# Conv transposes and query transposes later, one more empty step in the banded tail, raw output weights in general slots

## The chip, the cores and the metric

The kernel runs on one core of one Trainium2 chip, as one program without collectives. The metric is the device time of one execution in microseconds; the time before is the median of three executions, 1818.41 us (1817.18 to 1819.79). The engines of the core are TensorE (PE; its weight loads are listed as PEld), VectorE (DVE), ScalarE (ACT), GpSimd (POOL) and SyncE (SP), which here only issues DMAs. L709 means line 709 of the kernel before.

## The reference

Two layers of a backbone block over 1024 latent tokens and 256 context tokens, width 1024, all in float32:

```python
h  = rmsnorm(x, norm_w) * (1 + scale) + shift          # adaLN; the same for the context, hc
pl = split(h @ w_in)                                   # 14 parts: four branches and their gates
ya = softmax(q k^T) v   # A: latent attention, 4 heads, keys of context and latent tokens
yb = softmax(q k^T) v   # B: the same with rms-normed q, k; 4 heads, 2 key heads
yc = ...                # C: windowed: 128 tokens to either side, the context, and a sink term in the sum
yd = ...                # D: centred conv of 5 taps, silu, bidirectional state-space scan
x  = x + gate * (concat(ya, yb, yc, yd, each times silu of its gate) @ w_out)
```

The context gets the same update in the first layer only; the result is the final RMSNorm of x. In C the sink adds exp(sink) to the sum of exponentials by which the values are divided.

## The kernel before

Activations lie with features on partitions and tokens along the free axis, in three groups of tokens: the context (256) and two latent groups (512 each). Each float32 product is made of three passes of TensorE: operands are split into a high part (hi) and a low part (lo), and `mm3` adds hi·hi, lo·hi and hi·lo (L128, L129, L130). So each weight matrix that comes by DMA as raw float32 (`wfm_raw`, `wtm_raw`, `wo_raw`) is turned into hi by a cast and into lo by a subtraction before TensorE can use it.

A layer runs in this order: the input projection as a list of jobs (`in_proj`), the state-space branch spread over them, attention (branch 1, then 0, then 2; each with two pairs of heads), and the output projection (`out_proj`).

**Flushes.** Work that needs TensorE but depends on another engine is not issued at once. It is put on a list `soon` as `[delay, function]`. After each group of products `flush` issues the entries whose delay is 0 or less, to stand behind the group's last product, and takes 1 off the others. A conv job ends in `conv_fin`: VectorE adds five taps into cv (for the latent tokens) and cvc (context), ScalarE and VectorE make cth from them (L701, L702), and `turn` transposes cth in blocks of 128 on TensorE (L709, to ps_sxt), copies it to xbt on ScalarE (L711) and stores it (L712). A conv has ten such blocks. A `tm` job makes queries, keys and values with tokens on partitions; each pair of token tiles has a second half of its work, whose transposes (L781, to ps_qkt) wait for POOL's qkv (L736). It runs three pairs behind; the three that are left at the end go onto `soon` (L1029).

**Attention.** A unit is one branch, one pair of heads and one token group. It goes through blocks of keys: scores (ps_st), exponential to P on ScalarE (L1231), values (ps_acc, L1239); VectorE and POOL add the P's to ac (L1248, L1254). Beside it, for a later unit, scores in the other layout (ps_s) are reduced to maxima mp (L1148), which the softmax needs as a shift. What a unit still has to do is its tail, a list of steps that the next unit's blocks take, one for each block, or two while the list has more than six (in `main`): the output copy, two empty steps, `token_sums` (ps_sum, L1300; then asum, with a reciprocal, L1309), an empty step, and `finish`, which transposes the reciprocals (ps_rt, L1313), sends them through DRAM to be spread over partitions (rb) and multiplies (y, L1323). TensorE's order in attention is that of the program; other engines' orders come from the scheduler's estimates.

**Buffers.** `Slot` takes one of 35 general places of 4 KB a partition, freed by hand. `bg` is a ring of six such buffers, shared by P, by raw weights, and by the split outputs yh and yl.

**Output weights.** There are eight. In the last units of a layer `late(keep)` gives four steps per weight: issue the load (if enough slots are free), nothing, then two halves of cast and subtraction on VectorE (L1571, L1572). `out_proj` fetches what is missing with `split_w` (L288 to L292: DMA, cast on ScalarE, subtraction on VectorE).

Of the kernel before, what the change touches and what calls it, by code (L numbers as in the profile page):

```python
# [17 lines left out]
P = 128  # L18
# [39 lines left out]
def hybrid_block(ctx, tc, x, ctxt, c_t, w_fm, w_tm, w_mod, b_gate, p_col, p_row, w_qu, w_kvu, w_out,  # L58
# [572 lines left out]
    def in_proj(L, ht, need_ctx, side, follow, both, begun, make_last):  # L631
# [51 lines left out]
        def conv_fin(i, xp, has_ctx):  # L683
            xl, xc = xp
            w = halfw[:, i * 5:(i + 1) * 5]
            vl = Slot([P, NLAT], F32, "cv")
            parts = [(xl.t, vl.t, NLAT)]
            if has_ctx:
                parts.insert(0, (xc, tm((P, NCTX), name="cvc"), NCTX))
            for src, v, n in parts:  # L690
                nc.vector.tensor_scalar(out=v, in0=src, scalar1=w[:, 2:3], scalar2=halfb[:, i:i + 1],
                                        op0=ALU.mult, op1=ALU.add)
                for d in (-2, -1, 1, 2):
                    a, b = max(0, -d), n - max(0, d)
                    nc.vector.scalar_tensor_tensor(out=v[:, a:b], in0=src[:, a + d:b + d], scalar=w[:, d + 2:d + 3],
                                                   in1=v[:, a:b], op0=ALU.mult, op1=ALU.add)
            xl.free()
            for (lo, n) in (GROUPS if has_ctx else GROUPS[1:]):
                v = parts[0][1] if lo < NCTX else vl.t[:, lo - NCTX:lo - NCTX + n]
                th = tm(name="cth")  # L700
                nc.scalar.activation(out=th[:, :n], in_=v, func=AF.Tanh)  # L701
                nc.vector.scalar_tensor_tensor(out=th[:, :n], in0=th[:, :n], scalar=1.0, in1=v, op0=ALU.add, op1=ALU.mult)  # L702
                if i >= 2:
                    nc.sync.dma_start(out=d_xbc[i][:, lo:lo + n], in_=th[:, :n])
                if i < 4:
                    def turn(th=th, lo=lo, n=n):
                        pst = ps("S2", name="ps_sxt")
                        for t in range(n // P):
                            nc.tensor.transpose(pst[:, t * P:(t + 1) * P], th[:, t * P:(t + 1) * P], ident)  # L709
                        tt = tm(name="xbt")  # L710
                        nc.scalar.copy(tt[:, :n], pst[:, :n])  # L711
                        nc.sync.dma_start(out=d_xbt[i][:, lo:lo + n], in_=tt[:, :n])  # L712
                    soon.append([0, turn])
            vl.free()

        halfw = const([P, 30])
# [244 lines left out]
        for ji, j in enumerate(jobs):  # L961
            if ji < 2:
                continue
            w, nxt = nxt, None
            if j[4] is not None:
                j[4]()
            if ji + 1 < len(jobs):
                nxt = fetch(L, jobs[ji + 1])
            pieces, units = [], 0
            if ji >= len(jobs) - 2:  # L970
                if ji == len(jobs) - 2:
                    flush(ins, True)
                    for f in up:
                        f()
                    while side:
                        side.pop(0)()
                    first = follow(res)
                first.pop(0)()
                if ji == len(jobs) - 1:
                    pieces, units = first, 8 * len(j[2])  # L980
            if j[0] in ("fm", "conv"):
                def each():
                    nonlocal units
                    for _ in range(-(-len(pieces) // units) if units else 0):
                        pieces.pop(0)()
                    units -= 1

                if j[0] == "conv":
                    xp, ev = conv_prep(j[3], GROUPS[0] in j[2])
                else:  # L990
                    ev = j[3]
                for lo, n in j[2]:
                    if todo:
                        run(-(-len(todo) // n_ssd))
                        n_ssd -= 1
                    p, ins = products(ht, w, lo, n, "S2" if pieces else "MX", each)
                    ev(lo, n, p)
                    if side and SIDE0 <= ji < SIDE1:
                        side.pop(0)()
                    flush(ins)  # L1000
                if j[0] == "conv":
                    conv_fin(j[3], xp, GROUPS[0] in j[2])
                if side and ji >= 14:
                    side.pop(0)()
            else:
                whi = [u[0].t.rearrange("p (k c) -> p k c", c=256) for u in w]
                wlo = [u[1].t.rearrange("p (k c) -> p k c", c=256) for u in w]
                pend, due = [], 0
                for ti, t in enumerate(j[2][::2]):
                    p = ps("MX", name="ps_tm")  # L1010
                    for u in range(2):
                        for k in range(8):
                            ins = mm3(p[:, u * 256:u * 256 + 256], hh[k].tile(t + u), hl[k].tile(t + u),
                                      whi[k // 4][:, k % 4, :], wlo[k // 4][:, k % 4, :], k == 0, k == 7)
                    pend.append(tm_pair(j[1][0], j[1][1], t, p))
                    if ti >= 1:
                        pend[-2][0]()
                    if ti >= THIRD:
                        with tc.issue_after(ins.ins):
                            pend[-1 - THIRD][1]()  # L1020
                    flush(ins)
                    if side:
                        side.pop(0)()
                    due += UP_RATE.get(ji, 0)
                    while due >= 1 and up:
                        due -= 1
                        up.pop(0)()
                pend[-1][0]()
                soon.extend([0, f[1]] for f in pend[-THIRD:])  # L1029
            for u in w:  # L1030
                free_all(u)
            if j[5] is not None:
                j[5]()
# [4 lines left out]
    def attention(L, res, need_ctx, y, late, ahead):  # L1038
# [164 lines left out]
        def main(op, gi, steps, tail):  # L1203
# [107 lines left out]
            def finish():  # L1311
# [9 lines left out]
                    nc.sync.dma_start(out=rb[h * 64:h * 64 + 64, :n],  # L1321
                                      in_=dr[h * nt:(h + 1) * nt, :].rearrange("t q -> (t q)").unsqueeze(0).to_broadcast([64, n]))
                nc.vector.tensor_tensor(out=y[br * 2 + op["pair"]](lo, n), in0=rb[:, :n], in1=o[:, :n], op=ALU.mult)  # L1323
            return tail + [output, idle, idle, lambda: [token_sums(h) for h in range(2)], idle, finish]

        def idle():
            pass
# [202 lines left out]
    for L in range(DEPTH):  # L1530
        need_ctx = L < DEPTH - 1
        if L > 0:
            both, begun = [fetch(L, j) for j in first_two], {}
            ht = [], [], []
            add_half(ht)
            add_half(ht)
            for g in order(L)[:2]:
                for part in range(4):
                    make_ht(L, xs, ht, {}, g, part)

        def make_last():
            for part in range(4 if L else 0):
                make_ht(L, xs, ht, {}, order(L)[2], part)

        side = mod_g
        if L + 1 < DEPTH:
            load_params(L + 1)
            a, mod_g = mod_steps(L + 1)
            side = side + a
        else:  # L1550
            side = list(side)
        y, wo, gen, y_pairs = {}, [], [], {}

        def ahead():
            y_pairs[2] = y_pair(y, 2)

        def late(keep):

            st = []

            def first():
                if len(wo) < 8 and len(free_slots) >= 2 + keep:
                    raw = bg(name="wo_raw")
                    nc.sync.dma_start(out=raw, in_=w_out[L, len(wo)])
                    st.extend([raw, Slot([P, 1024], F32R, "wo_hi"), Slot([P, 1024], F32R, "wo_lo")])
                    wo.append(st[1:])

            def half(j):
                if st:
                    js = slice(j * 512, (j + 1) * 512)  # L1570
                    nc.vector.tensor_copy(st[1].t[:, js], st[0][:, js])  # L1571
                    nc.vector.tensor_tensor(out=st[2].t[:, js], in0=st[0][:, js], in1=f32(st[1].t[:, js]), op=ALU.subtract)  # L1572
            return [first, lambda: None, lambda: half(0), lambda: half(1)]

        def follow(res):
            for i in range(2):
                y[6 + i] = res["ssd"].y[i]
            gen.append(attention(L, res, need_ctx, y, late, ahead))
            return next(gen[0])

        res = in_proj(L, ht, need_ctx, side, follow, both, begun, make_last)
        y_slots, tail = next(gen[0])
        xs = out_proj(L, y, need_ctx, wo, tail, y_slots + res["ssd"].y_slots, y_pairs)
# [85 lines left out]
```

## Time and profile before

| | |
|---|---|
| median of 3 executions | 1818.41 us |
| the profiled execution | 1815.12 us, of it 1813.3 in the span of the trace |
| mean granted TensorE clock | 0.985 of full speed |
| busy: PE, DVE, POOL, ACT | 1718.6, 1141.4, 785.7, 734.4 us |
| DMA | 231.61 MB moved, 128 GB/s in the mean |

Busy times of engines overlap. PE is busy 95% of the span; what a change can take away lies in the rest, or in stretches where the clock is lower. The profile of this one execution says where. All durations below are from it; its time stands 3.3 us under the median.

### The profile page before, as it was taken

How to read it: one execution, taken by the hardware profiler on the slowest of the kernel's cores; microseconds unless marked ns; L12 is line 12 of the kernel's file. 1: busy time of each engine (PE TensorE's matmuls, PEld its weight loads, DVE VectorE, ACT ScalarE, POOL GpSimd, SP SyncE). 2: the span in 40 equal slices, each digit the busy share in tenths (PEclk: the TensorE clock that was granted, in tenths of full speed). 3: DMA queues.
4: the chain of work that ended last, by engine and by line, in shares of the span. 5: the costliest groups of instructions: out<-in, count | busy, mean ns of one | idle time of the engine just before them, and what ended most of it. 6: DMA issues, size and time to landing. Idle time of an engine off the chain costs nothing.

```text
span 1813.3 us, 27884 instructions
## 1 busy us (share of the span) xinstructions
PE 1718.6 (95%) x9658; PEld 1340.2 (74%) x9658; DVE 1141.4 (63%) x2294; ACT 734.4 (40%) x2048; POOL 785.7 (43%) x735
## 2 busy tenths in 40 slices
PE   6999999999989999998999889999999999999798
PEld 4667888899976566675787668888998656666586
DVE  6866965274347665668545677862753777656853
ACT  5432434333224554555423333343322355555431
POOL 2312643042325767665323233540342477666522
PEclk9999999999999999999999989999999999999999
DMA  9474333156566331322511434241668643221521
GB/s 317 142 235 138 123 103 125 50 191 197 190 181 167 109 101 35 99 81 88 185 59 41 132 120 140 82 146 39 205 186 258 175 120 89 56 67 36 172 74 58
DMA packets 130480, 231.61 MB, mean 128 GB/s; under 512 B 13826, under 2 KB 74628, under 8 KB 130340
## 3 DMA queue, kind: packets, MB, share of 16 engines
q1 hardware_dynamic: 130340, 229.84, 40.8%
q8 instruction: 76, 1.25, 0.3%
q14 instruction: 64, 0.52, 0.1%
HBM read 161.23 MB, written 68.45 MB: 127 GB/s over the span
## 4 chain that ended last, share of the span: by engine, by line
PE 71%; DVE 13%; DMA 5%; POOL 4%; issue 4%; ACT 2%; SPq 1%; POOLq 0%; DVEq 0%; ACTq 0%
PE ps_acc L1239 9%; PE ps_fm L128 7%; PE ps_fm L130 7%; PE ps_fm L129 7%; PE ps_s L1144 5%; PE ps_o L130 3%; PE ps_o L129 3%; PE ps_o L128 3%; PE ps_st L1227 3%; PE ps_st L1230 2%; PE ps_st L1222 2%; PE ps_st L1224 2%; PE ps_st L1223 2%; PE ps_tm L128 2%; PE ps_tm L129 2%
## 5 line engine op out<-in xcount | busy, mean ns | idle before, releaser
L1254 POOL TENSOR_TENSOR ac<-ac,P 128x512 f32<-128x512 f32 (+3 forms) x248 | 305.4, 1250 | 139.7 <-ACT P L1231 97.7
L1231 ACT ACTIVATE P<-ps_st 128x512 f32<-128x512 f32 (+3 forms) x456 | 244.3, 553 | 229.2 <-PE ps_st L1230 106.2
L1148 DVE TENSOR_REDUCE mp<-ps_s 128x1 f32<-128x512 f32 (+3 forms) x428 | 259.2, 656 | 112.2 <-PE ps_s L1144 106.6
L128 PE MATMUL ps_fm<-hh,wfm_hi 128*128 128x512 f32 x576 | 235.4, 409 | 8.3 <-DVE rb L734 5.0
L130 PE MATMUL ps_fm<-hl,wfm_hi 128*128 128x512 f32 x576 | 232.4, 404 | 1.5 <-POOL hl L405 0.7
L129 PE MATMUL ps_fm<-hh,wfm_lo 128*128 128x512 f32 x576 | 231.1, 401 | 0.0
L128 PE MATMUL ps_tm<-wtm_hi,hh 128*128 128x256 f32 x512 | 146.9, 287 | 0.6 <-ACT va L872 0.6
L129 PE MATMUL ps_tm<-wtm_hi,hl 128*128 128x256 f32 x512 | 146.0, 285 | 0.0
L130 PE MATMUL ps_tm<-wtm_lo,hh 128*128 128x256 f32 x512 | 145.7, 285 | 0.0
L128 PEld LDWEIGHTS ps_fm<-hh,wfm_hi 128*128 128x128 f32 x576 | 110.3, 191 | 31.7 <-issue 8.1
L130 PEld LDWEIGHTS ps_fm<-hl,wfm_hi 128*128 128x128 f32 x576 | 109.8, 191 | 27.4 <-POOL hl L405 3.2
L1254 DVE TENSOR_TENSOR ac<-ac,P 128x512 f32<-128x512 f32 (+3 forms) x88 | 96.2, 1094 | 48.7 <-ACT P L1231 23.7
L129 PEld LDWEIGHTS ps_fm<-hh,wfm_lo 128*128 128x128 f32 x576 | 110.1, 191 | 19.6 <-issue 0.8
L1248 POOL TENSOR_TENSOR ac<-P 128x1024 f32<-128x1024 f32 (+1 forms) x30 | 69.8, 2325 | 112.2 <-ACT P L1231 92.6
L129 PE MATMUL ps_o<-wo_hi,yl 128*128 128x512 f32 x288 | 112.6, 391 | 2.0 <-DVE yl L1404 1.9
L128 PE MATMUL ps_o<-wo_hi,yh 128*128 128x512 f32 x288 | 112.5, 391 | 0.0
L130 PE MATMUL ps_o<-wo_lo,yh 128*128 128x512 f32 x288 | 112.2, 390 | 0.0
L128 PEld LDWEIGHTS ps_tm<-wtm_hi,hh 128*128 128x128 f32 x512 | 98.7, 193 | 2.7 <-issue 1.6
L130 PEld LDWEIGHTS ps_tm<-wtm_lo,hh 128*128 128x128 f32 x512 | 98.6, 193 | 0.7 <-issue 0.4
L129 PEld LDWEIGHTS ps_tm<-wtm_hi,hl 128*128 128x128 f32 x512 | 98.7, 193 | 0.5
L1239 PE MATMUL ps_acc<-P,vt 128*64 128x512 f32 (+3 forms) x416 | 82.8, 525 | 4.1 <-ACT P L1231 4.1
L1227 PE MATMUL ps_st<-qq,kk 128*128 128x512 f32 (+3 forms) x208 | 82.2, 395 | 3.7 <-DVE mp L1148 3.6
(342 smaller groups left out, 4100.3 us busy)
## 6 DMA issues: line engine op xcount, KB each, us to landing
wfm_raw<-in_w_fm_dram SPq DMA_DIRECT2D x36, 512.0 KB
wm<-in_w_mod_dram SPq DMA_DIRECT2D x64, 256.0 KB
d_q<-qkhl SPq DMA_DIRECT2D x18, 512.0 KB
wm<-in_w_mod_dram SPq DMA_DIRECT2D x16, 512.0 KB
d_gate<-th SPq DMA_DIRECT2D x32, 256.0 KB
wtm_raw<-in_w_tm_dram SPq DMA_DIRECT2D x16, 512.0 KB
qq<-d_q SPq DMA_DIRECT2D x32, 256.0 KB
wo_raw<-in_w_out_dram SPq DMA_DIRECT2D x16, 512.0 KB
```

The source lines that it names most:

```text
L128: mm(o, lhsT=lh, rhs=rh, start=first, stop=False)
L129: mm(o, lhsT=ll, rhs=rh, start=False, stop=False)
L130: return mm(o, lhsT=lh, rhs=rl, start=False, stop=last)
L1144: mm(o, lhsT=qh(lo + t * P, P, 0, km), rhs=kh(k0, w, 0, km), start=True, stop=mo is None)
L1148: nc.vector.tensor_reduce(out=dst, in_=p[:, :nu * w].rearrange("p (u k) -> p u k", u=nu), axis=AX.X, op=ALU.max)
L1222: mm(st, lhsT=k(k0, 96), rhs=q(q0, 96), start=True, stop=False)
L1223: mm(st, lhsT=k(k1, 96), rhs=q(q0, 96), start=False, stop=False)
L1227: mm(st, lhsT=k(k0, 128), rhs=q(q0, 128), start=True, stop=False)
L1231: nc.scalar.activation(out=pts[:, h, :w], in_=st, func=AF.Exp, scale=op["scale"])
L1239: mm(acc[h * 64:h * 64 + 64, c0:c0 + w], lhsT=op["v"].tile(kb)[:, v0:v0 + 64], rhs=pts[:, h, :w], start=(bi == 0), stop=(bi == len(blocks) ...
L1248: nc.gpsimd.tensor_tensor(out=s[:, :, :n], in0=sums[0][:, :, :n], in1=pts[:, :, :n], op=ALU.add)
L1254: eng.tensor_tensor(out=s[:, h, c0:c0 + w], in0=s[:, h, c0:c0 + w], in1=pts[:, h, :w], op=ALU.add)
```

## The change

Four edits. `turn` is put on `soon` with a delay of 1 instead of 0, so a conv's transposes come one group of products later. The last three entries of a `tm` job get delays of 0, 1 and 2 instead of 0 each. In branch 2, the banded one, the tail has one more empty step before `finish`. And a late output weight's raw copy takes a general slot instead of a `bg` buffer, held until the second half is subtracted; its load is issued if three slots (instead of two) are free beyond those kept.

```diff
--- before.py
+++ after.py
@@ -710,7 +710,7 @@
                         tt = tm(name="xbt")
                         nc.scalar.copy(tt[:, :n], pst[:, :n])
                         nc.sync.dma_start(out=d_xbt[i][:, lo:lo + n], in_=tt[:, :n])
-                    soon.append([0, turn])
+                    soon.append([1, turn])
             vl.free()
 
         halfw = const([P, 30])
@@ -1026,7 +1026,7 @@
                         due -= 1
                         up.pop(0)()
                 pend[-1][0]()
-                soon.extend([0, f[1]] for f in pend[-THIRD:])
+                soon.extend([d, f[1]] for d, f in enumerate(pend[-THIRD:]))
             for u in w:
                 free_all(u)
             if j[5] is not None:
@@ -1321,7 +1321,7 @@
                     nc.sync.dma_start(out=rb[h * 64:h * 64 + 64, :n],
                                       in_=dr[h * nt:(h + 1) * nt, :].rearrange("t q -> (t q)").unsqueeze(0).to_broadcast([64, n]))
                 nc.vector.tensor_tensor(out=y[br * 2 + op["pair"]](lo, n), in0=rb[:, :n], in1=o[:, :n], op=ALU.mult)
-            return tail + [output, idle, idle, lambda: [token_sums(h) for h in range(2)], idle, finish]
+            return tail + [output, idle, idle, lambda: [token_sums(h) for h in range(2)], idle] + [idle] * (br == 2) + [finish]
 
         def idle():
             pass
@@ -1559,17 +1559,19 @@
             st = []
 
             def first():
-                if len(wo) < 8 and len(free_slots) >= 2 + keep:
-                    raw = bg(name="wo_raw")
-                    nc.sync.dma_start(out=raw, in_=w_out[L, len(wo)])
+                if len(wo) < 8 and len(free_slots) >= 3 + keep:
+                    raw = Slot([P, 1024], F32, "wo_raw")
+                    nc.sync.dma_start(out=raw.t, in_=w_out[L, len(wo)])
                     st.extend([raw, Slot([P, 1024], F32R, "wo_hi"), Slot([P, 1024], F32R, "wo_lo")])
                     wo.append(st[1:])
 
             def half(j):
                 if st:
                     js = slice(j * 512, (j + 1) * 512)
-                    nc.vector.tensor_copy(st[1].t[:, js], st[0][:, js])
-                    nc.vector.tensor_tensor(out=st[2].t[:, js], in0=st[0][:, js], in1=f32(st[1].t[:, js]), op=ALU.subtract)
+                    nc.vector.tensor_copy(st[1].t[:, js], st[0].t[:, js])
+                    nc.vector.tensor_tensor(out=st[2].t[:, js], in0=st[0].t[:, js], in1=f32(st[1].t[:, js]), op=ALU.subtract)
+                    if j:
+                        st[0].free()
             return [first, lambda: None, lambda: half(0), lambda: half(1)]
 
         def follow(res):
```

What it does to the order of instructions is shown at three places. First TensorE, second conv of layer 1: ps_sxt are the conv's transposes, ps_fm the products of the projection with hh and hl the split activations (hh_cx: context), ps_modg a piece of the modulation. Before:

```order
L129 MATMUL ps_fm<-hh_10256,wfm_lo 128x512
L130 MATMUL ps_fm<-hl_10261,wfm_hi 128x512
L269 MATMUL ps_modg<-wm,con 32x512 x4
L709 MATMUL ps_sxt<-con,cth 128x128 x10
L128 MATMUL ps_fm<-hh_10243,wfm_hi 128x512
L129 MATMUL ps_fm<-hh_10243,wfm_lo 128x512
L130 MATMUL ps_fm<-hl_10248,wfm_hi 128x512
```

and now (the numbers of hh and hl are given anew by each build):

```order
L130 MATMUL ps_fm<-hl_10259,wfm_hi 128x512
L269 MATMUL ps_modg<-wm,con 32x512 x4
L128 MATMUL ps_fm<-hh_10241,wfm_hi 128x512
L129 MATMUL ps_fm<-hh_10241,wfm_lo 128x512
...
L129 MATMUL ps_fm<-hh_10254,wfm_lo 128x512
L130 MATMUL ps_fm<-hl_10259,wfm_hi 128x512
L709 MATMUL ps_sxt<-con,cth 128x128 x10
L128 MATMUL ps_fm<-hh_cx,wfm_hi 128x256
L129 MATMUL ps_fm<-hh_cx,wfm_lo 128x256
```

The ten transposes stood at the head of a group of 24 products, and now stand behind it. The next is VectorE in layer 0's banded branch, up to the reciprocal of the second unit's sums: wo are the output weights, mp maxima, y an output step. Before:

```order
L1571 CAST wo_hi<-wo_raw 128x512 x2
L1572 TENSOR_TENSOR wo_lo<-wo_raw,wo_hi 128x512 x2
L1571 CAST wo_hi<-wo_raw 128x512 x2
L1572 TENSOR_TENSOR wo_lo<-wo_raw,wo_hi 128x512 x2
L1148 TENSOR_REDUCE mp<-ps_s 128x2 x2
L1148 TENSOR_REDUCE mp<-ps_s 128x1
L1571 CAST wo_hi<-wo_raw 128x512 x2
L1572 TENSOR_TENSOR wo_lo<-wo_raw,wo_hi 128x512 x2
L1323 TENSOR_TENSOR y_8290<-rb,o 128x512
L1306 SCALAR_TENSOR_TENSOR asum<-es,asum 128x8
L1148 TENSOR_REDUCE mp<-ps_s 128x1
L1309 RECIPROCAL asum<-asum 128x8
```

and now:

```order
L1572 TENSOR_TENSOR wo_lo<-wo_raw,wo_hi 128x512 x2
L1571 CAST wo_hi<-wo_raw 128x512 x2
L1148 TENSOR_REDUCE mp<-ps_s 128x2 x2
L1148 TENSOR_REDUCE mp<-ps_s 128x1
L1572 TENSOR_TENSOR wo_lo<-wo_raw,wo_hi 128x512 x2
L1323 TENSOR_TENSOR y_8290<-rb,o 128x512
L1306 SCALAR_TENSOR_TENSOR asum<-es,asum 128x8
L1148 TENSOR_REDUCE mp<-ps_s 128x1
L1309 RECIPROCAL asum<-asum 128x8
```

The unit's reciprocal had six casts and six subtractions ahead of it here, and now has two and four; the others stand further up, in the global branch. The last is TensorE in layer 0's output projection; ps_o are its banks, the seventh and eighth weight are 9096 and 9347 before, of which only 9347 was fetched late:

```order
L130 MATMUL ps_o_9424<-wo_lo_8752,yh_9255 128x512
L129 MATMUL ps_o_9377<-wo_hi_9067,yl_9256 128x512
L130 MATMUL ps_o_9377<-wo_lo_9068,yh_9255 128x512
L128 MATMUL ps_o_9377<-wo_hi_9096,yh_9255 128x512
L129 MATMUL ps_o_9377<-wo_hi_9096,yl_9256 128x512
L130 MATMUL ps_o_9377<-wo_lo_9097,yh_9255 128x512
L128 MATMUL ps_o_9377<-wo_hi_9347,yh_9255 128x512
L129 MATMUL ps_o_9377<-wo_hi_9347,yl_9256 128x512
L130 MATMUL ps_o_9377<-wo_lo_9348,yh_9255 128x512
L128 MATMUL ps_o_9424<-wo_hi_8797,yh_9255 128x512
```

and now they are 9339 and 9345, both fetched late:

```order
L129 MATMUL ps_o_9375<-wo_hi_9088,yl_9248 128x512
L130 MATMUL ps_o_9375<-wo_lo_9089,yh_9247 128x512
L128 MATMUL ps_o_9375<-wo_hi_9339,yh_9247 128x512
L129 MATMUL ps_o_9375<-wo_hi_9339,yl_9248 128x512
L130 MATMUL ps_o_9375<-wo_lo_9340,yh_9247 128x512
L128 MATMUL ps_o_9375<-wo_hi_9345,yh_9247 128x512
L129 MATMUL ps_o_9375<-wo_hi_9345,yl_9248 128x512
L130 MATMUL ps_o_9422<-wo_lo_8752,yh_9247 128x512
L128 MATMUL ps_o_9422<-wo_hi_9000,yh_9247 128x512
L129 MATMUL ps_o_9422<-wo_hi_9000,yl_9248 128x512
L130 MATMUL ps_o_9375<-wo_lo_9346,yh_9247 128x512
```

The eighth weight's products have moved apart: its low part is used after three products of the other bank.

## Rows read from the trace of the kernel before

**Rows 1.** Page, part 4: the chain that ended last, share of the span.

```profile
PE 71%; DVE 13%; DMA 5%; POOL 4%; issue 4%; ACT 2%; SPq 1%; POOLq 0%; DVEq 0%; ACTq 0%
```

**Rows 2.** Waits of TensorE: what waited for what; total us, times, longest us.

```profile
PE ps_sxt L709 <- DVE cth L702: 13.7, 7, 3.7
...
PE ps_rt L1313 <- DVE asum L1309: 10.3, 7, 4.5
...
PE ps_qkt L781 <- POOL qkv L736: 5.3, 5, 1.7
...
PE ps_sxt L709 <- ACT xbt L711: 0.4, 1, 0.4
```

**Rows 3.** Timeline around conv transposes: start, us, engine, line; in brackets idle before.

```profile
89.23 0.62 PE L709 MATMUL ps_sxt<-con,cth 128*128 128x128 f32 x2 [2.37 <-DVE cth L702]
...
146.71 1.70 PE L709 MATMUL ps_sxt<-con,cth 128*128 128x128 f32 x8 [2.28 <-DVE cth L702]
...
1056.63 2.12 DVE L702 SCALAR_TENSOR_TENSOR cth<-cth,cv 128x512 f32<-128x512 f32 x2
...
1056.76 0.69 PE L709 MATMUL ps_sxt<-con,cth 128*128 128x128 f32 x2 [3.71 <-DVE cth L702]
...
1066.30 0.28 PE L128 MATMUL ps_fm<-hh_cx,wfm_hi 128*128 128x256 f32 x1
```

**Rows 4.** Stretches at half clock, convs: length, busy PE, PEld, DVE, ACT, POOL, clock, DMA, GB/s.

```profile
1055.32:1062.15 6.83, 4.96 (x16) 3.87 (x17) 6.76 (x10) 4.52 (x10) 4.39 (x5) 0.50 0.35 132
...
sum 17.06, PE 15.10 PEld 12.13 DVE 10.65 ACT 9.52 POOL 4.39; mean PE 3.78 PEld 3.03 DVE 2.66 ACT 2.38 POOL 1.10
```

**Rows 5.** Timeline: a transpose of queries that keeps its place.

```profile
1395.92 0.44 PE L781 MATMUL ps_qkt<-con,qkv 128*128 128x128 f32 x2 [1.67 <-POOL qkv L736]
```

**Rows 6.** VectorE by line, 820.2 to 833.7: busy, mean ns; and the timeline there.

```profile
L1572 DVE TENSOR_TENSOR wo_lo<-wo_raw,wo_hi 128x512 fp32r<-128x512 f32 x6 | 4.9, 858 | 0.0
...
L1571 DVE CAST wo_hi<-wo_raw 128x512 fp32r<-128x512 f32 x6 | 3.9, 684 | 0.0
...
829.87 2.64 POOL L1248 TENSOR_TENSOR ac<-P 128x1024 f32<-128x1024 f32 x1 [3.64 <-issue]
...
830.24 2.82 DVE L1323 TENSOR_TENSOR y<-rb,o 128x512 f32<-128x512 f32 x1
...
833.86 0.37 PE L1313 MATMUL ps_rt<-con,asum 128*8 128x128 f32 x1 [4.51 <-DVE asum L1309]
```

**Rows 7.** Two of three stretches at half clock in the banded branch, columns as rows 4.

```profile
830.03:836.86 6.83, 3.00 (x14) 3.03 (x15) 5.72 (x9) 1.02 (x3) 2.48 (x1) 0.50 0.00 1
...
1683.37:1686.78 3.41, 3.41 (x12) 3.41 (x13) 3.41 (x8) 0.78 (x2) 0.93 (x1) 0.50 0.49 156
```

**Rows 8.** Timeline: one of three transposes of reciprocals.

```profile
870.46 0.27 PE L1313 MATMUL ps_rt<-con,asum 128*8 128x128 f32 x1 [1.34 <-DVE asum L1309]
```

**Rows 9.** Timeline: late output weight of layer 0, and the product that needs the seventh.

```profile
864.17 0.33 SPq L288 DMA_DIRECT2D wo_raw<-in_w_out_dram  x1
...
869.14 1.09 ACT L291 CAST wo_hi<-wo_raw 128x1024 fp32r<-128x1024 f32 x1
...
870.79 1.22 DVE L292 TENSOR_TENSOR wo_lo<-wo_raw,wo_hi 128x1024 fp32r<-128x1024 f32 x1
...
873.32 0.39 PE L128 MATMUL ps_o<-wo_hi,yh 128*128 128x512 f32 x1
```

**Rows 10.** Layer 1, band: a stretch of 10 us as in rows 4; timeline.

```profile
1650.00:1660.00 10.00, 10.00 (x65) 6.87 (x64) 4.49 (x9) 6.24 (x28) 4.64 (x7) 1.00 0.06 18
...
1683.21 0.47 PE L1227 MATMUL ps_st<-qq,kk 128*128 128x256 f32 x1 [2.69 <-DVE mp L1148]
...
1705.89 0.66 ACT L1231 ACTIVATE P<-ps_st 128x256 f32<-128x256 f32 x2 [4.75 <-DVE wo_lo L1572]
...
1706.33 0.92 PE L1239 MATMUL ps_acc<-P,vt 128*64 128x256 f32 x4 [4.10 <-ACT P L1231]
```

**Rows 11.** Subtractions of raw output weights: ns min/median/max.

```profile
L1572 DVE TENSOR_TENSOR wo_lo<-wo_raw,wo_hi x30: 675/679/2835, 821.4 to 1717.2; 128x512 fp32r<-128x512 f32 x30
```

## Prediction

> **What bounds the kernel now.** I read the chain of waits first: 71% of what ended last is TensorE, 13% VectorE [rows 1]. So a gap on TensorE, or a stretch in which it runs at its lower clock, is what can give time back. Next comes the list of what TensorE waited for [rows 2]. Three kinds of entry belong to this change: transposes behind a convolution (ps_sxt) that wait for cth, transposes of queries and keys (ps_qkt) that wait for qkv, and transposes of reciprocal sums (ps_rt) that wait for asum. Last I read the timeline around each gap, for what the late engine was doing, and the tables of the stretches at the lower clock. The execution in the trace took 1815.1 us, 3.3 under the median of 1818.4; a difference worked out in the trace is taken off the median.
>
> **Conv transposes.** The ten transposes of a conv now stand one group of products later. The first conv of layer 0 keeps its place in the order, so its 2.37 us stays [rows 3]. What can go is 13.7 − 2.4 + 0.4 (the wait for a copied block, at one of the same places) = 11.7 us [rows 2, 3]. The largest piece is the 3.71 us at 1056.76. There the last cth is done at 1056.63 + 2.12 = 1058.75, and the new place, behind 24 more products, is where the next group's first product with hh_cx starts, at 1066.30: 7.5 us to spare [rows 3]. Read in the same way, the other places have a cushion too, and what pulls TensorE forward pulls the conv's inputs forward with it. No instruction is new: the copy to xbt on ScalarE and the store to d_xbt on SyncE follow the transposes, and their readers come much later. In layer 1 ScalarE has four TA activations ahead of such a copy now; I put 1.0 us against that.
>
> In and behind four of these gaps the granted clock is 0.50, that is 1.2 instead of 2.4 GHz, for 17.06 us, in which TensorE works 15.10 [rows 4]. At the upper level that work takes half as long: 7.55 us. Smaller gaps stay nearby, so I take 6.0. Conv: 11.7 + 6.0 − 1.0 = 16.7. Bounds: 2.3, if only the 2.28 us in layer 0 [rows 3] goes, because VectorE works 6.76 of 6.83 us around layer 1's largest gap [rows 4]; and 11.7 + 7.6 = 19.3.
>
> **Query and key transposes.** The last three pairs of a job no longer come all at the first flush, but at three. The list has 5.3 us in five waits [rows 2]; the 1.67 at 1395.92 belongs to a transpose that stays [rows 5], and so does one of 0.2. The rest, 3.4, gets a further group of products or two in front of it. I take 3.4; it is 0 if POOL's part is as late there.
>
> **Sums and reciprocals, layer 0.** A banded unit's tail gets one more empty step; but two steps are taken at once while more than six are left. So in layer 0 two ps_rt move back by one block and one pair of sums moves forward, and in layer 1 ps_rt stays and three pairs of sums move forward by a block. The costliest wait, 4.51 us at 833.86, is for a transpose that does not move at all [rows 6]. What changes there is VectorE's queue: from 820.2 to 833.7 it holds six casts and six subtractions of output weights in front of the reciprocal [rows 6]. Of these, four casts and two subtractions go, since weights that have their raw copy in a general slot are begun in the global branch: 4 × 0.68 + 2 × 0.86 = 4.4 us; I take 4.0. Half the work in the stretch at half clock there, 3.00 / 2 = 1.5, may follow [rows 7]; I take 1.0. Of the other waits for asum [rows 2], three together are 3.7 us, of which one stands here [rows 8]: the first goes with sums a block earlier, the second with its transpose a block later, the third with seven fewer yl in front of its reciprocal. I take 3.0. Layer 0: 8.0, between 3.0 (those alone) and 4.5 + 1.5 + 3.7 = 9.7.
>
> **What it costs: layer 0's output projection.** A load now needs three free slots instead of two, so six weights are there when the projection starts, not seven, and two are fetched late. Before, the late one was asked for at 864.17, its cast began at 869.14, and its low part was done at 870.79 + 1.22 = 872.0; TensorE came to the seventh weight at 873.32 [rows 9]. With the gaps in front gone it gets there near 871.5: the seventh is just in time. The eighth is wanted 0.7 us later. Its load lands between 0.3 (the issue before it) and 5.0 us (one load after the other) behind the seventh's; then come ScalarE's 1.1, and VectorE's 1.2 behind a row of yl. That is 0 to 6 us of wait. I take 2.5, nearer to two loads side by side.
>
> **Layer 1, band.** The 4.10 us at 1706.33 is ps_acc waiting for P, and P waited 4.75 us for a low weight on VectorE [rows 10]: the exponential needs the buffer that a raw weight holds. With raw weights elsewhere this goes. The 2.69 at 1683.21 is a maximum behind casts [rows 10]; of the eight weights four are now cast ahead of the first banded sums, where VectorE works 4.49 of 10 us [rows 10]. Behind each of the two lie 3.41 us of work at half clock, of which one stands in [rows 7]; twice the half of it, 3.4, can follow. Of 4.1 + 2.7 + 3.4 = 10.2 I take 8.5; the lower bound is 4.1. The sums that come a block earlier should find the adds they need done: nothing.
>
> **A rule on the casts.** The row: a subtraction of 128x512 takes 679 ns in the median and 2835 at the longest [rows 11]; the output step at 830.24 took 2.82 us, and POOL's add beside it ran from 829.87 for 2.64 [rows 6]. The Trainium skill (SBUF — State Buffer, "Who interferes with whom") has it that a VectorE instruction with two SBUF inputs and a GpSimd one that reads SBUF take one port pair in turn, and that the second is fully blocked. The trace agrees. By that rule, casts moved to where POOL adds all the time would be dear. In my sum they cost what the medians say and are hidden by the free time of VectorE there; the other value makes the third rival.
>
> **Sum.** 16.7 + 3.4 + 8.0 − 2.5 + 8.5 = 34.1 us; 1818.4 − 34.1 = 1784.3. All upper values: 19.3 + 3.4 + 9.7 − 0 + 10.2 = 42.6, which is 1776. All lower: 2.3 + 0 + 3.0 − 6.0 + 4.1 = 3.4, which is 1815.
>
> **Rivals.**
> - *The waits move on.* TensorE arrives earlier and finds VectorE late at its next need. Then layer 0's conv gives 2.3, the query transposes 3.4, layer 0's band half, 4.0, the projection takes 2.5, and layer 1 gives its 4.1: 11.3 us, 1807. For it: VectorE is second on the chain [rows 1] and full in places [rows 4]. Against: between those places it has stretches with time to spare [rows 10].
> - *The clock does not come back.* Idle time goes, but other gaps keep the lower level: 34.1 less the clock's 6.0, 1.0 and what 8.5 holds above 6.8, 1.7: 25.4, 1793. Against: each stretch at 0.50 begins at one of the waits that go.
> - *Casts behind POOL's adds (slower).* Ten casts and subtractions in layer 0 and sixteen in layer 1 move into the global branch, ahead of maxima for which TensorE does not wait there now. If eighteen of the 26 meet an add and lose 2.835 − 0.679 = 2.16 us each with TensorE behind them, that is 39 us: 1818.4 − 34.1 + 39 = 1823. It decides from 34.1 / 26 = 1.3 us for each on average. Against: VectorE works less than half the time there [rows 10], so a slow cast can lie in its idle time.
>
> **How the numbers follow.** Chances: forecast 0.55, clock 0.17, waits that move on 0.18, slow casts 0.06; 0.04 for a mixture that ends near no change. A measurement of this kernel can tell 0.2%, 3.6 us, from no change. Faster is the first two and 0.17 of the third, 0.89; same 0.05; slower 0.06. The range 1773 to 1810 holds these three but for their far ends; the forecast's own is 1776 to 1794.
>
> **What would show it.** In the new profile ps_sxt waits for cth only once, some 2.4 us, and the clock stays at 1.00 around the later conv transposes; ps_rt of the unit at 834 waits less than 1 us; P in layer 1 waits for no weight; ps_o in layer 0 has a new wait of 1 to 4 us for wo. I am wrong if ps_s or ps_st waits for mp in the global branches, if ps_o waits for wo by more than 6 us, or if ps_sxt waits for ScalarE where it waited for VectorE.

## The result, and the profile after

The changed kernel takes 1790.2 us (median of four executions, 1787.1 to 1792.6) against 1817.8 before (1815.5 to 1819.8): ratio 0.9853, 95% interval 0.984 to 0.9866. That is 26.7 us by the ratio; 34.1 were forecast, with a range of 1773 to 1810. The profiled execution took 1792.6, the slowest of the four; its span is 22.5 us shorter than that of before.

How those 22.5 us are made up stands in part 1 of the page, the busy time of TensorE, before and after:

```profile
PE 1718.6 (95%) x9658; PEld 1340.2 (74%) x9658; DVE 1141.4 (63%) x2294; ACT 734.4 (40%) x2048; POOL 785.7 (43%) x735
```

```profile
PE 1713.7 (96%) x9658; PEld 1334.7 (75%) x9658; DVE 1137.0 (63%) x2291; ACT 731.3 (41%) x2049; POOL 786.8 (44%) x735
```

The same 9658 products are 4.9 us shorter in sum; the mean granted clock is 0.990 where it was 0.985. TensorE's idle time goes from 1813.3 − 1718.6 = 94.7 to 1790.8 − 1713.7 = 77.1: 17.6 us.

The list of what TensorE waited for, after (total us, times, longest):

```profile
...
PE ps_k L129 <- DVE wku L284: 4.8, 2, 3.3
PE ps_k L128 <- DMA c<-d_c: 3.2, 2, 3.0
PE ps_s L1144 <- DVE mp L1148: 3.1, 4, 1.4
PE ps_sxt L709 <- DVE cth L702: 3.0, 3, 2.3
PE ps_fm L128 <- ACT wfm_hi L291: 2.7, 1, 2.7
PE ps_rt L1313 <- DVE asum L1309: 2.7, 4, 1.1
PE ps_cum L449 <- DVE s L446: 2.5, 1, 2.5
...
PE ps_qkt L781 <- POOL qkv L736: 1.9, 2, 1.0
```

Beside [rows 2]: ps_sxt went from 13.7 to 3.0 us, ps_rt from 10.3 to 2.7, ps_qkt from 5.3 to 1.9. One entry is new, ps_cum (sums in the state-space branch, 2.5 us), and ps_k (latent keys) stands at 8.0 us, where before it was 1.7.

To see where the time goes, I took each instruction of TensorE that both traces have and subtracted its start in the one from its start in the other. This lead grows or falls by stage, in us:

| stage (us of before) | changed | conv alone | queries alone | step alone | slots alone | step and slots |
|---|---|---|---|---|---|---|
| 80–160, convs of layer 0 | +6.9 | +6.4 | +0.5 | −0.9 | +0.2 | +3.2 |
| 380–480, queries, layer 0 | +2.1 | −0.6 | +2.3 | +1.7 | +2.8 | +2.2 |
| 480–540 | −3.4 | +0.2 | +0.8 | −1.4 | +1.4 | +1.1 |
| 815–890, band and projection, layer 0 | +7.0 | −1.9 | −0.5 | −0.1 | +2.0 | +7.7 |
| 1020–1110, convs of layer 1 | +8.3 | +9.8 | +1.0 | −1.1 | −0.7 | +0.7 |
| 1270–1400, queries, layer 1 | −1.6 | +0.7 | −2.4 | +0.6 | 0.0 | −0.1 |
| 1640–1720, band, layer 1 | +7.3 | 0.0 | +0.2 | −2.4 | +2.2 | +5.6 |

Entries up to about 3 us in stages that a kernel does not touch are what one execution differs from another by. At 480 the order of the instructions differs between the kernels, so the rows 380–480 and 480–540 are best read as one sum: −1.3 for the changed kernel, +3.1 for the queries alone. The seven entries of the changed kernel add up to 26.6 us; the stages that are not listed take 4.1 of them back.

### The profile page after: what moved, and what is told of

Its sections match the earlier page's. It is cut to its first block, busy times and chain, and to the rows that moved or that the text cites. A ratio compares the mean times of both kernels' runs of the same rounds, so it can differ in the third digit from the quotient of the medians.

```text
span 1790.8 us, 27801 instructions
## 1 busy us (share of the span) xinstructions
PE 1713.7 (96%) x9658; PEld 1334.7 (75%) x9658; DVE 1137.0 (63%) x2291; ACT 731.3 (41%) x2049; POOL 786.8 (44%) x735
## 4 chain that ended last, share of the span: by engine, by line
PE 52%; DVE 11%; DMA 4%; POOL 2%; issue 2%; ACT 2%; SPq 0%; POOLq 0%; DVEq 0%; ACTq 0%
PE ps_acc L1239 8%; PE ps_s L1144 4%; PE ps_fm L129 3%; PE ps_fm L130 3%; PE ps_fm L128 3%; PE ps_o L130 3%; PE ps_o L128 3%; PE ps_o L129 3%; PE ps_st L1227 3%; PE ps_st L1230 2%; PE ps_st L1222 2%; DVE mp L1148 2%; PE ps_st L1223 2%; PE ps_st L1224 2%; PE ps_tm L128 1%
## 5 line engine op out<-in xcount | busy, mean ns | idle before, releaser
L130 PEld LDWEIGHTS ps_fm<-hl,wfm_hi 128*128 128x128 f32 x576 | 109.5, 190 | 28.9 <-POOL hl L405 4.5
L1248 POOL TENSOR_TENSOR ac<-P 128x1024 f32<-128x1024 f32 (+1 forms) x30 | 65.9, 2198 | 117.1 <-ACT P L1231 99.7
L1448 POOL TENSOR_TENSOR xres<-xres,dl 128x512 f32<-128x512 f32 x32 | 42.4, 1326 | 95.6 <-DVE dl L1447 92.4
```

What stands on the lines that cost most here:

```text
L130: return mm(o, lhsT=lh, rhs=rl, start=False, stop=last)
L1248: nc.gpsimd.tensor_tensor(out=s[:, :, :n], in0=sums[0][:, :, :n], in1=pts[:, :, :n], op=ALU.add)
L1448: (nc.vector if t == ts[-1] else nc.gpsimd).tensor_tensor(out=xt.t[:, js], in0=xt.t[:, js], in1=d, op=ALU.add)
```

## The experiments

**Each part alone.** Three kernels make one edit each:

```diff
-                    soon.append([0, turn])
+                    soon.append([1, turn])
```

> Only the conv transposes move, everything else as before. By the prediction this part is worth 16.7 us: ratio 0.991. By the lead that TensorE has in the two traces at the same instruction, it is worth 6.9 us in layer 0 and 8.4 in layer 1, 15.3: ratio 0.9915, and layer 1's first conv gives nothing, because a wait of about 2.5 us of ps_cum for s stands where ps_sxt waited for cth. A rival: these places were only late because other parts stood as they did, and the part alone gives half, 7 to 8 us.

Measured: 0.9911 (0.9895 to 0.9926), 16.2 us. The full amount, not half; layer 1's first conv has the ps_cum wait.

```diff
-                soon.extend([0, f[1]] for f in pend[-THIRD:])
+                soon.extend([d, f[1]] for d, f in enumerate(pend[-THIRD:]))
```

> Only the query and key transposes are spread over three flushes. By the prediction: 3.4 us faster, ratio 0.998. By the lead of TensorE between the traces: the stretches with these jobs lose 1.3 us in layer 0 and 1.6 in layer 1, so about 3 us slower, ratio 1.0015, with new waits of ps_k for wku (3.3 us near 402) and for c (3.0 us near 1298 less the lead). Rival: the new waits come from the other edits (TensorE arriving earlier), and this part alone is 3 us faster without them.

Measured: 1.0017 (1.0001 to 1.0034), 3.1 us slower, an interval that nearly reaches no change. The rival falls: the new waits are there with this edit alone, from the timeline of TensorE:

```profile
408.08 0.39 PE L129 MATMUL ps_k<-c,wku 128*128 128x256 f32 x1 [3.22 <-DVE wku L284]
...
1302.74 0.47 PE L128 MATMUL ps_k<-c,wku 128*128 128x256 f32 x2 [2.79 <-DMA c<-d_c]
```

With the transposes out of the way, the order puts the first ps_k (latent keys) further forward on TensorE. There their weights and their input have not come. But other waits go with the edit, and not only those of ps_qkt (5.3 us to 1.8). Of TensorE's waits before

```profile
PE ps_fm L128 <- DVE rb L734: 5.0, 1, 5.0
...
PE ps_q L128 <- DMA c<-d_c: 3.3, 2, 2.3
...
PE ps_k L128 <- DMA c<-d_c: 1.7, 2, 1.0
```

the first (products of the projection, behind the rotation of queries and keys on VectorE; its rb is not that of attention) is gone and the second is 0.4; ps_k grows to 9.0 and ps_fm waits 2.0 for wfm_hi. So in this trace 11.4 us of waits go and 9.3 come. Its execution took 1814.9 us, less than the 1817.4 of the median before, so this trace does not show where the median's 3.1 us are lost.

```diff
-            return tail + [output, idle, idle, lambda: [token_sums(h) for h in range(2)], idle, finish]
+            return tail + [output, idle, idle, lambda: [token_sums(h) for h in range(2)], idle] + [idle] * (br == 2) + [finish]
```

> Only the empty step in the banded branch; raw output weights stay in the ring. By the prediction two of layer 0's waits for asum go, 1.3 + 1.0 us, the 4.5 us at 833.9 and layer 1's waits stay: 2 us faster, ratio 0.999. Rival: the step alone does nothing, within 1 us, since VectorE's casts stand in front of the reciprocal wherever the transpose is.

Measured: 0.9998 (0.9986 to 1.001). Nothing, the amount that its rival named. The rival's reason does not hold: TensorE's waits for asum in ps_rt did fall, from 10.3 to 7.7 us, by about the 2.3 that were priced, but in the same trace its waits for mp in ps_s rose from 2.1 to 6.6.

The fourth kernel has the general slots alone (the last hunk of the change):

```diff
-                if len(wo) < 8 and len(free_slots) >= 2 + keep:
-                    raw = bg(name="wo_raw")
+                if len(wo) < 8 and len(free_slots) >= 3 + keep:
+                    raw = Slot([P, 1024], F32, "wo_raw")
```

> Only the raw output weights in general slots. By the prediction: layer 0's 4.0 + 1.0 and the third reciprocal's 1.0, less 2.5 for the projection, and layer 1's 8.5: 12 us, ratio 0.9934. By the lead between the traces the two band edits together give 6.8 + 7.1 = 13.9, of which 12 to 14 are this one: ratio 0.993. Rival: the gain needs the empty step as well, and this part alone gives under 6 us.

Measured: 0.9957 (0.9941 to 0.9974), 7.8 us: between the two.

**The parts in company.** The step alone and the slots alone give 8 us, while the two traces put 14 into the banded branches. So I ran the two together (the edits of the third and the fourth kernel, nothing else), and the changed kernel without the step (the edit of the third taken back):

> Only the general slots and the empty step, the rest as before. If the two need each other, 14 us: ratio 0.9923. If they add as they did alone, 8 us: 0.9956.

Measured: 0.9913 (0.9886 to 0.994), 15.8 us. The step, which gave nothing alone, is worth 15.8 − 7.8 = 8.0 us beside the slots.

> The changed kernel without the empty step in the banded branch. Alone the step gave nothing (0.9998), alone the general slots gave 7.8 us of the 14 that the two traces show in the banded branches. If the two need each other, this is 6 us slower than the changed kernel: ratio 0.9888, and in layer 1 a transpose of reciprocals waits about 4 us for asum where ps_acc waited for P. Rival: the step does nothing here either, ratio 0.9853.

Measured: 0.9874 (0.9844 to 0.9903), 3.8 us above 0.9853, with overlapping intervals, so the price of the step in this company is not settled. In its trace ps_rt waits 3.28 us in layer 1 and 3.62 in layer 0, so the waits that the step removes are the same.

Why, is read in the timelines. Layer 1, slots alone, then changed; the rows are SyncE's DMA queue, VectorE, POOL and TensorE:

```profile
1692.71 0.46 SPq L1318 DMA_DIRECT2D d_rs<-rrow  x1
...
1696.45 2.54 POOL L1248 TENSOR_TENSOR ac<-P 128x1024 f32<-128x1024 f32 x1
...
1696.80 2.73 DVE L1572 TENSOR_TENSOR wo_lo<-wo_raw,wo_hi 128x512 fp32r<-128x512 f32 x1
...
1699.57 0.34 SPq L1417 DMA_DIRECT2D fw<-in_fnw_dram  x1
1700.00 1.15 SPq L1321 DMA_DIRECT2D rb<-d_rs  x2
...
1705.80 0.69 DVE L1323 TENSOR_TENSOR y<-rb,o 128x512 f32<-128x512 f32 x1 [4.99 <-DMA rb<-d_rs]
1706.41 0.16 DVE L1306 SCALAR_TENSOR_TENSOR asum<-es,asum 128x8 f32<-128x8 f32 x1
...
1706.86 0.35 PE L1313 MATMUL ps_rt<-con,asum 128*8 128x128 f32 x1 [4.10 <-DVE asum L1309]
```

```profile
1678.05 0.46 SPq L1318 DMA_DIRECT2D d_rs<-rrow  x1
1679.55 1.15 SPq L1321 DMA_DIRECT2D rb<-d_rs  x2
1681.16 0.35 SPq L1417 DMA_DIRECT2D fw<-in_fnw_dram  x1
...
1687.23 0.95 DVE L1323 TENSOR_TENSOR y<-rb,o 128x512 f32<-128x512 f32 x1
...
1689.08 0.27 PE L1313 MATMUL ps_rt<-con,asum 128*8 128x128 f32 x1 [0.75 <-DVE asum L1309]
```

The 4.10 us for P [rows 10] are gone with the slots, but 4.10 for asum come in their place. The reciprocals are stored at 1692.71, but rb, which reads them back, is issued at 1700.00, right behind the load of the final norm's weights (fw) at 1699.57. What holds up fw is the edit of the slots itself: fw takes a general slot, and SyncE stands at it for 6.3 us, until the last subtraction of a raw weight is done at 1696.80 + 2.73 = 1699.53. That subtraction, beside POOL's add, takes 2.73 us where the median is 0.68. The output step y waits for rb, and asum of the next unit stands behind y on VectorE. The changed kernel without the step has the same 6.3 us. With the empty step the order has rb ahead of fw, 1.5 us behind the store, and the chain is in time. So the step, which moves no ps_rt in this layer, works through the order of a DMA queue. This is read from the traces with and without the step; no run moves fw alone.

Layer 0, slots alone, then changed; POOL's add and the small sum asum on VectorE:

```profile
826.98 2.34 POOL L1248 TENSOR_TENSOR ac<-P 128x1024 f32<-128x1024 f32 x1 [3.61 <-issue]
...
827.04 2.30 DVE L1306 SCALAR_TENSOR_TENSOR asum<-es,asum 128x8 f32<-128x8 f32 x1
...
830.06 0.37 PE L1313 MATMUL ps_rt<-con,asum 128*8 128x128 f32 x1 [3.61 <-DVE asum L1309]
```

```profile
824.77 0.15 DVE L1306 SCALAR_TENSOR_TENSOR asum<-es,asum 128x8 f32<-128x8 f32 x1
...
825.09 2.38 POOL L1248 TENSOR_TENSOR ac<-P 128x1024 f32<-128x1024 f32 x1 [4.00 <-issue]
...
825.64 0.27 PE L1313 MATMUL ps_rt<-con,asum 128*8 128x128 f32 x1 [1.08 <-DVE asum L1309]
```

A sum of 128x8 elements takes 2.30 us where it starts 0.06 us behind POOL's add, and 0.15 where it starts ahead of it. In the kernel before it is the output step that meets this add: 2.82 us at 830.24 [rows 6], where in the changed kernel it takes 0.68.

**The query transposes in company.** The changed kernel with the edit of the second kernel taken back:

> The changed kernel without the edit of the query and key transposes (all three at the first flush, as before). If that edit costs time by itself, as it did alone (ratio 1.0017), this is about 3 us faster than the changed kernel: ratio to before 0.9836, 1787. Rival: in company the earlier TensorE meets other transfers there and the loss comes from these, then this is not faster than 0.9853.

The changed kernel with that edit in layer 0 (L = 0) only:

```diff
-                soon.extend([d, f[1]] for d, f in enumerate(pend[-THIRD:]))
+                soon.extend([0 if L else d, f[1]] for d, f in enumerate(pend[-THIRD:]))
```

> The changed kernel, but with the query and key transposes spread in layer 0 only. By the lead between the traces layer 0 wins 2 us with the spreading up to 480 and layer 1 loses 3: 1787, ratio 0.983, between this and the kernel without the edit. Rival: the two layers do not differ, and it is as the changed kernel, 0.9853.

And the changed kernel as it is, beside it:

> The changed kernel once more, beside the two others on the same chip: 0.9853 again; a ratio within 0.002 of that of the kernel with spreading in layer 0 only would leave open which of the two is faster.

Measured: without the edit 0.9839 (0.981 to 0.9868), in layer 0 only 0.9839 (0.982 to 0.9858), the changed kernel again 0.9843 (0.9822 to 0.9865). In company the edit's cost can't be told from nothing. The traces show the same exchange of waits as above: from the kernel without the edit to the changed one, ps_k rises from 0.8 to 8.0 us, and ps_fm for wfm_hi (2.7) and ps_tm for ka (1.6) come; ps_fm for rb (4.0) goes, ps_q falls from 3.4 to 0.8 and ps_qkt from 5.3 to 1.9. That is 11.5 against 10.0.

**The wait that came at layer 1's first conv.** After, in the changed kernel, and with the conv edit alone:

```profile
1023.74 1.54 PE L449 MATMUL ps_cum<-s,con 128*128 128x80 f32 x6 [2.48 <-DVE s L446]
```

```profile
1030.47 0.87 PE L449 MATMUL ps_cum<-s,con 128*128 128x80 f32 x6 [2.48 <-DVE s L446]
```

In the changed kernel without the query edit I split the function at ps_cum and put its second half on the same list:

```diff
             ssd.decays(dt_raw)
+            soon.append([2, ssd.decays_rest])
             free_all(dt_slots)
```

> The kernel without the edit of the query transposes, and the second half of the state-space decays (from ps_cum on) two flushes later, beside the first conv's transposes in layer 1. If the 2.48 us of ps_cum waiting for s, with 3 to 7 us at half clock behind it, is what took back layer 1's first conv, it goes: 2.5 + 1.7 to 3.4 = 4 to 6 us faster than without it, ratio 0.981. Rival: VectorE is so full there that another instruction waits as long, and nothing is gained.

Measured: 0.9832 (0.9801 to 0.9863), no gain over 0.9839. The wait of ps_cum goes, but at the layer's second conv there comes another:

```profile
1050.15 1.09 PE L713 MATMUL ps_sxt<-con,cth 128*128 128x128 f32 x4 [5.06 <-DVE grow L276]
```

I took its cause to be a bank shared with ps_modg, so the next kernel gives ps_cum a bank of the other ring (the expectation calls the place the first conv; it is the second):

```diff
-            pcum = ps("TR", name="ps_cum")
+            pcum = ps("S2", name="ps_cum")
```

> As the kernel with ps_cum two flushes later, but ps_cum takes its bank from the ring that ps_sxt uses instead of the one that ps_modg uses. There the wait at layer 1's first conv was 5.06 us for VectorE's grow, which reads ps_modg out of its bank. If ps_cum stood behind that bank, the wait falls under 1 us and the kernel gains 5 us plus 1.7 for the clock: about 1782, ratio 0.980. Rival: ps_sxt itself waited behind VectorE's queue, then the wait stays and the ratio is 0.983.

Measured: 0.9845 (0.9827 to 0.9863), and the wait of 5.06 us is still there. The bank is not the cause; what ps_sxt needs from VectorE there stays open. None of the runs is clearly faster than the changed kernel.

## Why the prediction was right, and where it was not

**Conv, 16.7 forecast, 16.2 measured alone.** The mechanism holds: ps_sxt now waits 2.29 us at the place that did not move (at 88.35) and 0.7 in two waits at 1064 and 1065; one wait in all was forecast. TensorE's clock, beside [rows 4], in stretches of the changed kernel (busy PE, PEld, DVE, ACT, POOL, then clock, DMA, GB/s):

```profile
140.00:150.00 10.00, 10.00 (x60) 7.21 (x58) 3.23 (x4) 4.83 (x9) 0.00 (x0) 1.00 0.67 210
1020.00:1030.00 10.00, 7.52 (x27) 4.64 (x26) 4.20 (x19) 1.26 (x6) 0.00 (x0) 0.67 0.17 52
1040.00:1050.00 10.00, 10.00 (x54) 7.47 (x53) 9.25 (x12) 5.93 (x13) 5.53 (x5) 1.00 0.47 171
1050.00:1060.00 10.00, 10.00 (x58) 8.77 (x57) 9.72 (x12) 1.29 (x3) 2.42 (x4) 1.00 0.18 66
1060.00:1070.00 10.00, 9.29 (x57) 7.71 (x56) 9.58 (x14) 5.32 (x13) 2.75 (x3) 1.00 0.36 132
```

The clock is back at three of the four places. At the fourth it is 0.50 from 1023.32 to 1030.15, behind the wait of ps_cum, in this execution twice as long as before. Two new stretches at 0.50, 3.41 us each, begin at 402.10 and 1299.80, at the waits of ps_k. The wait of ps_cum, and not ScalarE's TA activations, is what stood against the sum. So the 1.0 taken off was set against the wrong thing and was too small. In the trace of the conv edit alone 11.1 us of waits of ps_sxt and 5.3 of TensorE's work go and the 2.5 of ps_cum come, 13.9 together; that the measured 16.2 lies within 0.5 of the forecast is in part luck. VectorE at 9.25 and 9.72 of 10 us did not hold TensorE up, so the low bound for layer 1 was too careful.

**Query transposes, 3.4 forecast, 3.1 the other way alone, nothing in company.** This is the step that failed. The waits I counted did go: ps_qkt has two left. But I looked only at what was moved later. What the scheduler moved earlier in their place, ps_k, was not followed to its inputs, and the two waits that go besides, of ps_fm and ps_q, were not counted either. The edit is an exchange of some 10 us of waits against as much, not a gain of 3.4.

**Layer 0, 8.0 less 2.5 forecast, 7.0 by the lead.** The 4.51 us at 833.86 [rows 6] fell to 1.08, where less than 1 was forecast, and the three smaller waits went. But the split between edits was wrong: the shorter VectorE queue alone leaves 3.61 of it, and the rest is that asum comes ahead of POOL's add. Of the 4.51 some 2.1 were the meeting of the output step with that add; the prediction read this row for the casts, and not for the wait that it stands in. The cost was wrong too: the two late weights of the projection, whose first product starts at 853.98, in the timeline after:

```profile
851.24 0.36 SPq L288 DMA_DIRECT2D wo_raw<-in_w_out_dram  x1
...
851.86 1.15 SPq L1321 DMA_DIRECT2D rb<-d_rs  x2
...
853.17 0.46 SPq L288 DMA_DIRECT2D wo_raw<-in_w_out_dram  x1
...
857.73 1.05 ACT L291 CAST wo_hi<-wo_raw 128x1024 fp32r<-128x1024 f32 x1 [1.73 <-DMA wo_raw<-in_w_out_dram]
...
859.14 0.69 DVE L1323 TENSOR_TENSOR y<-rb,o 128x512 f32<-128x512 f32 x1 [2.71 <-DMA rb<-d_rs]
...
859.87 0.90 ACT L1403 CAST yh<-y 128x128 fp32r<-128x128 f32 x4 [0.34 <-DVE y L1323]
860.22 0.73 PE L128 MATMUL ps_o<-wo_hi,yh 128*128 128x512 f32 x2 [1.29 <-ACT yh L1403]
```

Before, the one late load was asked for 1.1 us ahead of the first product [rows 9]; now the first is 2.7 us ahead of it and the second 0.8. Their casts begin at 857.73 and 860.67, 2.9 us apart, and no product waits for a weight. So the loads overlapped, and of the 0 to 6 us for the weights themselves 0 came. The one gap, 1.29 us, is for yh, which waited on ScalarE for the output step y, and y waited for rb. This rb was issued between the two loads, and y began 7.3 us after its issue; with no load of a weight beside it, y began 3.7 us after the issue of rb (at 710.29 and 1504.49). So the two loads may have cost time here after all, by way of rb and not of the weights. No run settles it, and in a second execution of the changed kernel the gap is 0.2 us.

**Layer 1, 8.5 forecast, 7.3 by the lead.** The waits for P and for mp [rows 10] went; two shorter ones for mp came in ps_s, 2.4 us together. Wrong was that the sums a block earlier would do nothing: without them the first 4.1 us turn into a wait for asum.

**The slow casts** did not come in the changed kernel. Instructions on raw output weights after, ns min/median/max:

```profile
L1572 DVE TENSOR_TENSOR wo_lo<-wo_raw,wo_hi x28: 654/679/1776, 782.7 to 1683.8; 128x512 fp32r<-128x512 f32 x28
```

The longest is 1776 where it was 2835 [rows 11]; with the slots alone it was still 2734, and that one is the subtraction that fw waits for. The rule on the shared ports (the Trainium skill, SBUF — State Buffer, "Who interferes with whom") agrees with these traces, but the prediction aimed it at the many casts. What it decided over were single instructions in front of a wait: the sum of 128x8 in layer 0 and, without the step, the last subtraction in layer 1.

**The sum.** 34.1 forecast, 26.7 measured. The query transposes are the 3.4 that did not come. The rest of the difference, 4.0, is not placed: conv alone and step with slots, 16.2 and 15.8, gave 32.0, more than the 30.7 that the forecast had for them. With the 3.1 of the queries taken off they make 28.9, and the interval of the whole, 24.4 to 29.1 us, holds that.

## What to carry to other kernels

When work is moved later, read the order for what now stands earlier in its place, and follow that to its inputs on every queue. A wait that ends on a shared engine hides the one behind it: an edit can give nothing until another is there, so price such edits together and test them together. When a buffer is taken from another pool, ask who else takes from that pool and what stands behind it on the same queue: here a load waited for a slot, and a small load that the chain to TensorE needed stood behind it. And an estimate of 0 to 6 us between two loads deserves a look at how far loads of that size overlap in the same trace.

## What was not expected of the hardware

A VectorE instruction of 128x8 elements took 2.30 us where it started 0.06 us after a POOL add that ran for 2.34, and 0.15 where it started ahead of that add. The output step at 830.24 met the add with 2.27 us of it left and took 2.82 where it takes 0.68 elsewhere; the subtraction at 1696.80 met one with 2.19 left and took 2.73 where the median is 0.68. In these rows the price of the meeting, 2.05 to 2.15 us, is about what was left of the other engine's instruction, and not a matter of the own one's size.
